# One core, hybrid mixer and mixture of experts: two-head units on row tiles, halved exponentials, one bank for chunk output and state, another load order at the start

## The chip, the cores and the metric

One core of one Trainium2 chip runs the whole program. The metric is the time of one execution on the device in microseconds (us), as the median of three runs.

## What is computed

One layer on 1024 tokens of width 1024, all in float32. The projections are the sum of three products of two reduced parts each, so that they keep float32 accuracy.

```python
hq, hf, hi, hg, gq, gk, gv, ga, gg = jnp.split(x @ w_in, split_at, axis=-1)
f = lb + (1.0 - lb) * sigmoid(hf)
o_h = chunk_gla(hq * 128 ** -0.5, 1.0 - f, hi, log(f))          # 4 heads, keys of 128
log_a = log_sigmoid(ga @ w_a2 + b_a) / 16                        # ga has rank 16
o_g = chunk_gla(gq * 64 ** -0.5, gk, gv, log_a)                  # 4 heads, keys of 64
o = concat(rms(o_h) * norm_h * silu(hg), rms(o_g) * norm_g * silu(gg))
x = layer_norm(alpha * x + o @ w_out)
x = layer_norm(alpha * x + hierarchical_moe(x))                  # 64 experts, top 2

def chunk_gla(q, k, v, log_g):   # per head: S_t = diag(g_t) S_{t-1} + k_t v_t^T, o_t = q_t S_t
    b = cumsum(log_g)            # inside a chunk
    scores[t, s] = sum_k q[t, k] * exp(b[t, k] - b[s, k]) * k[s, k]      # s <= t
    o = scores @ v + (q * exp(b)) @ S_prev
    S = exp(b_last) * S_prev + (k * exp(b_last - b))^T @ v
```

## The kernel before

Three stages follow each other: the mixer, the output projection with the first norm and the router, and the experts, whose 402 MB of weights pass through a ring of eight buffers. VectorE (DVE), ScalarE (ACT), POOL (GpSimd) and the load queue SP are ordered by a scheduler when the program is built; the order of TensorE (PE) in the mixer is the program's own (line 642).

**Projections.** `queue` (lines 275 to 289) lists blocks of 128 columns of `w_in`. A block (`block`, line 168) computes 128 by 1024 outputs in two halves of 512 tokens, each with 24 matmuls: for each of 8 slices of the contraction the upper part of the weights times the upper part of x (line 176), the upper part times x's lower part (178), and the lower part times x's upper part (180). The block `ga` has 16 columns and takes the same 48 matmuls, with `gah` and `gal` as its weights. `weights` (139) loads the next block's weights and splits them: a rounded copy on ScalarE (155), the rest by a subtraction on VectorE (156). When a half block ends, its evacuation runs: keys to `k_of`, queries to `q_of`, values to `to_rows` (ScalarE copies them to the tile `vt`, line 217, TensorE turns them 20 matmuls later, 222), gates to `gated`. `fill(n)` issues the next n matmuls of the queue and stands between the steps of the recurrence, so that TensorE has work.

**Start.** `first_blocks` (291) loads x transposed, in eight parts of 128 tokens; the first four come in two halves each. `split_x` makes the rounded upper part `xh` on ScalarE (303) and the lower part `xl` on VectorE or POOL (304). The four last parts wait for the buffers of the first four. Then come the two halves of tokens (loop on n), each for two blocks (i); their matmuls are lines 327 to 329.

**Recurrence.** `gla` (397) handles a unit: units 0 to 3 are one head with keys of 128 rows, units 4 and 5 are two heads with keys of 64 rows each. `prepare` (364) makes the log decays `lg` and their sums `P` within chunks of 128 tokens, eight chunks per head. Scores inside a chunk are built in seven levels, which pair blocks of 1, 2, 4 up to 64 tokens. `level` (426) makes scaled keys and queries: two subtractions on POOL (471, 472), one exponential of 128 by 1024 on ScalarE (473), keys (436, or 454 for two heads) and queries (475) on VectorE. For two heads the keys lie in `K2`: each head has its own 32 columns of a block, with zeros in the other head's 64 rows, and one VectorE instruction per head writes them. `scores` (478) then issues matmuls of 32 by 32 results (485, 500), or the last level's (512 for one head, 518 for two), all with 128 rows of contraction; both heads' results lie in one bank. `masked` (417) puts the results of the first five levels together (422, 424).

**Chunks.** After the levels, line 591 loops over the chunks c: the output's part from the state (595), its part from scores (597), the state's update for chunk c + 1 (`state`, 574: matmul in 580, VectorE in 585 or 587), ScalarE's sum of squares (604) and VectorE's copy (605), then `fill(12)`. Output and state take buffers of the pool `ps_ou`, three banks, each a buffer of its own:

```python
            op = ps_ou.tile([128, W], F32, name="ou")
            if c:
                PE.matmul(op, QI[:, cs], states[c - 1][:, :W], start=True, stop=False)
...
            if c < NT - 2:
                state(c + 1)
...
                S.activation(junk, op[:, w], AF.Square, accum_out=ssq[hh][:, c:c + 1])
                V.tensor_copy(osb[hh][:, c], op[:, w])
            next(steps, None)
            fill(n_ch)
```

`next(steps)` runs a piece of the next unit's `prepare`. After the last unit, `fill(1000)` (695) issues the rest of the projections; buffers of the mixer then become those of the output projection's weights and of the first expert weights.

## Time and profile before

| | |
|---|---|
| median of three runs | 1590.79 us (1589.87 to 1592.31) |
| the profiled execution's own time | 1590.95 us |
| its span, first to last instruction | 1589.2 us |
| TensorE busy, over the span | 1428.5 us (90%) |
| VectorE | 782.0 us (49%) |
| ScalarE | 470.5 us (30%) |
| POOL | 401.7 us (25%) |
| mean granted TensorE clock | 0.958 of full speed |
| moved by DMA | 449.15 MB, mean 283 GB/s |

In the profile a matmul of float32 operands appears as two instructions. Matmuls are pipelined, so their durations overlap; the distance from one start to the next is what one costs in a row of them. A wait in brackets behind a row is idle time of that engine, with the instruction that ended it. Shares over the span are averages over stages with different limits; the rows below are from single stages.

### The profile page before, as it was taken

The page shows a single profiled execution, that of the slowest core. Times are in us where ns is not written, and L with a number is a line of the kernel's source. Part 1 is how long each engine was busy: PE and PEld are TensorE (multiplying, and loading weights), DVE is VectorE, ACT ScalarE, POOL GpSimd, SP SyncE. Part 2 cuts the span into 40 slices and gives each one's busy share as a digit, 9 for nine tenths or more (in the row PEclk, how much of TensorE's full clock was granted, in tenths as well). Part 3 has the DMA queues.
Part 4 walks back from the last instruction along what each step waited for, and adds up shares of the span by engine and source line. Part 5 has one row for each costly group of instructions (what it writes and reads, how often), then busy time and mean ns, then how long its engine had stood idle before and what let it go on. Part 6 is the DMA issues. An engine that isn't in the chain of part 4 may idle for free. (4 is left out here: it accounts for less than half of the span.)

```text
span 1589.2 us, 23253 instructions
## 1 busy us (share of the span) xinstructions
PE 1428.5 (90%) x9359; PEld 806.1 (51%) x9359; DVE 782.0 (49%) x1838; ACT 470.5 (30%) x948; POOL 401.7 (25%) x275
## 2 busy tenths in 40 slices
PE   7999999899999998979988989889998889899795
PEld 5777678677778884333333333333334334334332
DVE  5667645667766672435334354244344334433534
ACT  5546444545533243112112112112112112111210
POOL 4524323323202103112112213113113212321230
PEclk9999999999999999988999999998999999999998
DMA  5101011010137257999999999999999999999992
GB/s 167 42 33 35 29 34 35 28 35 28 33 99 307 75 191 300 425 426 426 424 425 427 425 426 426 426 425 427 425 427 426 426 426 426 422 423 425 424 389 84
DMA packets 61680, 449.15 MB, mean 283 GB/s; under 512 B 12160, under 2 KB 20608, under 8 KB 36608
## 3 DMA queue, kind: packets, MB, share of 16 engines
q1 hardware_dynamic: 50768, 430.01, 65.3%
q0 software_dynamic: 9216, 12.61, 2.2%
q10 hardware_dynamic: 1584, 5.01, 0.8%
q8 instruction: 74, 1.21, 0.3%
q14 instruction: 38, 0.31, 0.1%
HBM read 447.58 MB, written 20.97 MB: 295 GB/s over the span
## 5 line engine op out<-in xcount | busy, mean ns | idle before, releaser
L1151 PE MATMUL gu<-w1u,VOA 128*64 128x512 f32 x1024 | 237.1, 606 | 8.7 <-DMA w1u<-in_wu_dram 8.2
L1151 PE MATMUL gu<-w2u,VOA 128*64 128x512 f32 x1024 | 232.6, 599 | 8.1 <-DMA w2u<-in_wu_dram 8.1
L1036 DVE TENSOR_TENSOR sg<-sg,gu 128x512 f32<-128x512 f32 x32 | 22.0, 688 | 430.6 <-PE gu L1151 430.6
L1080 POOL TENSOR_TENSOR VOA<-VOA 128x1024 f32<-128x1024 f32 x32 | 81.1, 2534 | 368.4 <-PE tp L1026 367.0
L176 PE MATMUL pp<-xh,wh 128*128 128x512 f32 x416 | 172.9, 416 | 0.0
L178 PE MATMUL pp<-xl,wh 128*128 128x512 f32 x416 | 165.7, 398 | 0.0
L180 PE MATMUL pp<-xh,wl 128*128 128x512 f32 x416 | 164.7, 396 | 0.0
L1151 PEld LDWEIGHTS gu<-w1u,VOA 128*64 128x64 f32 x1024 | 80.5, 140 | 160.7 <-issue 139.2
L1151 PEld LDWEIGHTS gu<-w2u,VOA 128*64 128x64 f32 x1024 | 77.0, 139 | 157.8 <-issue 143.1
L1175 PE MATMUL yp<-w1u,hT 128*64 128x512 f32 x512 | 127.7, 656 | 0.0
L1175 PE MATMUL yp<-w2u,hT 128*64 128x512 f32 x512 | 122.2, 633 | 0.0
L1029 ACT ACTIVATE VOA<-tp,cols 128x128 f32<-128x128 f32 x256 | 93.0, 470 | 89.9 <-PE tp L1026 89.9
L1026 PE MATMUL tp<-cst,VOA 128*128 128x128 f32 x256 | 46.2, 330 | 77.6 <-DMA VOA<-x1d,gidx 75.5
L1046 ACT COPY hT<-tp 128x512 f32<-128x512 f32 x32 | 18.8, 586 | 326.3 <-PE tp L1044 326.3
L1011 POOL DMA_INDIRECT VOA<-x1d,gidx x32 | 32.5, 1015 | 299.5 <-DMA out_dram<-VOA,oidx 282.1
L471 POOL TENSOR_TENSOR d<-P 128x512 f32<-128x512 f32 x36 | 51.6, 1435 | 199.6 <-DVE ny L88 65.3
L1053 DVE SCALAR_TENSOR_TENSOR y<-yp,gcol,y 128x512 fp32r<-128x512 f32 x64 | 47.2, 748 | 99.5 <-ACT y L1052 99.2
L1052 ACT ACTIVATE y<-yp,gcol 128x512 fp32r<-128x512 f32 x64 | 44.0, 688 | 171.6 <-PE yp L1175 171.6
L176 PEld LDWEIGHTS pp<-xh,wh 128*128 128x128 f32 x416 | 78.9, 190 | 18.2 <-issue 1.9
L180 PEld LDWEIGHTS pp<-xh,wl 128*128 128x128 f32 x416 | 78.9, 190 | 17.3
L178 PEld LDWEIGHTS pp<-xl,wh 128*128 128x128 f32 x416 | 79.1, 190 | 13.6
L1081 POOL TENSOR_TENSOR VOA<-VOA 128x1024 f32<-128x1024 f32 x32 | 79.6, 2489 | 2.5
(272 smaller groups left out, 2213.6 us busy)
## 6 DMA issues: line engine op xcount, KB each, us to landing
w1u<-in_wu_dram SPq DMA_DIRECT2D x32, 2048.0 KB, 26.5
w1u<-in_wd_dram SPq DMA_DIRECT2D x32, 2048.0 KB, 27.8
w2u<-in_wg_dram SPq DMA_DIRECT2D x31, 2048.0 KB, 23.0
w1u<-in_wg_dram SPq DMA_DIRECT2D x30, 2048.0 KB, 22.0
w2u<-in_wd_dram SPq DMA_DIRECT2D x30, 2048.0 KB, 27.5
w2u<-in_wu_dram SPq DMA_DIRECT2D x30, 2048.0 KB, 24.1
wr<-in_wf_dram SPq DMA_DIRECT2D x36, 256.0 KB, 2.6
r<-in_x_dram SPq DMA_DIRECT2D x8, 512.0 KB, 3.7
```

Source lines behind the costliest of these rows:

```text
L176: PE.matmul(ps, hi[:, k], xh[:, k, ts], start=(k == 0), stop=False)
L178: PE.matmul(ps, hi[:, k], xl[:, k, ts], start=False, stop=False)
L180: PE.matmul(ps, lo[:, k], xh[:, k, ts], start=False, stop=(k == KT - 1))
L471: G.tensor_tensor(ev[:, :, 0], ref, Pv[:, :, 0], OP.subtract)
L1026: PE.transpose(tp[:, i], sv[:, half * 4 + i], ident)
L1029: S.activation(xt[:, c], tp[:, i], AF.Identity, bias=cols[:, 42 + c:43 + c], scale=cols[:, 34 + c:35 + c])
L1052: S.mul(yh[:, ns], yps[n], gate_col)
L1053: V.scalar_tensor_tensor(yl[:, ns], yps[n], gate_col, yh[:, ns], op0=OP.mult, op1=OP.subtract)
L1080: E.tensor_tensor(o, o, ln1[0], OP.mult)
L1081: E.tensor_tensor(o, o, ln1[1], OP.add)
L1151: PE.matmul(dst[64 * b:64 * b + 64], xt[:, c, 64 * b:64 * b + 64], utile[6 * p + u + b][:, c], start=(c == 0), stop=(c == KT - 1))
L1175: PE.matmul(yps[n][64 * b:64 * b + 64], hT[:, c, 64 * b:64 * b + 64], utile[6 * p + 4 + b][:, c, n * 512:(n + 1) * 512], start=(c == 0), s ...
```

## The change

The gate block's two weights become one tile of 32 columns, upper and lower part side by side; its product with x's upper and lower part gives 32 rows, which the low-rank matmul sums, as its weights are there twice. `vt` gets a second buffer. Two-head units keep keys and queries in the one-head layout; each head's score matmuls read its 64 rows alone and write a bank of its own (`banks`), one of them from `ps_ou`. The exponential of a level is done in halves, and the keys are made between POOL's two subtractions in the program. Chunk output and the next state's matmul share one buffer of `ps_ou`. At the start, the first halves of four x parts come before their second halves, the first block's weights between them; two of the four upper parts are made on VectorE, all eight lower ones too, after the upper ones; and the first blocks use x's lower part after all products with its upper part. The unchanged rest of each part is left out here.

```diff
-    gah = mc.tile([128, KT, 16], F32R, name="gah")
-    gal = mc.tile([128, KT, 16], F32R, name="gal")
+    gahl = mc.tile([128, KT, 32], F32R, name="gahl")
...
-    zt = g2.tile([128, 512], F32, name="vt", bufs=1)[:, 0:256].bitcast(BF)
+    zt = g2.tile([128, 512], F32, name="vt", bufs=2)[:, 0:256].bitcast(BF)
...
-    K2 = [pers.tile([128, NT * 4, 2, 32], F32, name=f"K2{i}") for i in range(2)]
-    Kb = [k_.rearrange("p b h s -> p (b h s)")[:, :T] for k_ in K2]
+    Kb = [pers.tile([128, T], F32, name=f"Kb{i}") for i in range(2)]
...
-            (S if i == 0 else nc.sync).dma_start(rs[j], queue[i][0][:, j * m:j * m + m])
+            (S if i == j == 0 else nc.sync).dma_start(rs[j], queue[i][0][:, j * m:j * m + m])
...
             for k in range(KT):
-                PE.matmul(ps, hi[:, k], xh[:, k, ts], start=(k == 0), stop=False)
-                yield
-                PE.matmul(ps, hi[:, k], xl[:, k, ts], start=False, stop=False)
-                yield
-                PE.matmul(ps, lo[:, k], xh[:, k, ts], start=False, stop=(k == KT - 1))
-                if k == KT - 1:
-                    queue[i][1](ps, ts)
-                yield
+                terms = [(hi, xh), (hi, xl)] + ([(lo, xh)] if lo is not None else [])
+                for j, (w, x_) in enumerate(terms):
+                    PE.matmul(ps, w[:, k], x_[:, k, ts], start=(k == 0 and j == 0),
+                              stop=(k == KT - 1 and j == len(terms) - 1))
+                    if k == KT - 1 and j == len(terms) - 1:
+                        queue[i][1](ps, ts)
+                    yield
...
-        def load(q, parts):
-            xr[q] = g2.tile([128, KT, 128], F32, name=("osb", "d")[q % 2])
-            for i in range(parts):
-                ks = slice(i * KT // parts, (i + 1) * KT // parts)
-                nc.sync.dma_start(xr[q][:, ks], xT_in[q][:, ks])
-
-        def split_x(q, i, parts, E):
+        def load(q, i, parts):
+            if i == 0:
+                xr[q] = g2.tile([128, KT, 128], F32, name=("osb", "d")[q % 2])
+            ks = slice(i * KT // parts, (i + 1) * KT // parts)
+            nc.sync.dma_start(xr[q][:, ks], xT_in[q][:, ks])
+
+        def upper(q, i, parts, copy):
             ks, ts = slice(i * KT // parts, (i + 1) * KT // parts), slice(q * 128, (q + 1) * 128)
-            S.copy(xh[:, ks, ts], xr[q][:, ks])
-            E.tensor_tensor(xl[:, ks, ts], xr[q][:, ks], xh[:, ks, ts], OP.subtract)
-
-        s0 = weights(0, raw=g1.tile([128, KT, 128], F32, name="lg"), parts=2)
-        for q in range(4):
-            load(q, 2)
-        s1 = weights(1, raw=g1.tile([128, KT, 128], F32, name="P"))
-        s0()
+            return copy(xh[:, ks, ts], xr[q][:, ks])
+
+        def lower(q, i, parts, E):
+            ks, ts = slice(i * KT // parts, (i + 1) * KT // parts), slice(q * 128, (q + 1) * 128)
+            return E.tensor_tensor(xl[:, ks, ts], xr[q][:, ks], xh[:, ks, ts], OP.subtract)
+
+        l0, s0 = weights(0, raw=g1.tile([128, KT, 128], F32, name="lg"), parts=2)
+        for i in range(2):
+            for j, q in enumerate(range(4)):
+                if (i, j) in ((0, 1), (1, 0)):
+                    l0(i)
+                load(q, i, 2)
+        l1, s1 = weights(1, raw=g1.tile([128, KT, 128], F32, name="P"))
+        l1(0), l1(1)
+        for i in range(2):
+            s0(i)
+            for q in range(4):
+                up = upper(q, i, 2, S.copy if q < 2 else V.tensor_copy)
         for i in range(2):
             for q in range(4):
-                split_x(q, i, 2, V if q < 3 else G)
+                order(lower(q, i, 2, V), up, "the upper parts go first")
         for q in range(4, 8):
-            load(q, 1)
+            load(q, 0, 1)
             if q == 4:
-                s1()
-            split_x(q, 0, 1, V if q % 2 else G)
+                s1(0), s1(1)
+            upper(q, 0, 1, S.copy)
+            lower(q, 0, 1, V if q % 2 else G)
...
-                    PE.matmul(ps, hi[:, k], xl[:, k, ts], start=False, stop=False)
-                    PE.matmul(ps, lo[:, k], xh[:, k, ts], start=False, stop=(k == KT - 1))
+                    PE.matmul(ps, lo[:, k], xh[:, k, ts], start=False, stop=False)
+                for k in range(KT):
+                    PE.matmul(ps, hi[:, k], xl[:, k, ts], start=False, stop=(k == KT - 1))
...
-        for t_ in K2 + Qb + Ab + Sg:
+        for t_ in Kb[1:] + Qb[1:] + Ab + Sg:
...
-                r = slice(32 * n, 32 * n + 16)
+                r = slice(32 * n, 32 * n + 32)
...
         if h0 == 4:
-            for k_ in K2:
-                for hh in range(nh):
-                    G.memset(k_[(1 - hh) * dk:(2 - hh) * dk, :, hh], 0.0)
...
-        def masked(sps, li, first):
+        def masked(sps, li):
             m = slice(32 * li, 32 * li + 32)
-            a, s_ = acc.rearrange("p c u t -> p (c u) t"), sps.rearrange("p c u t -> p (c u) t")
-            shape = [128, NT * nh, 32]
-            if first:
-                V.tensor_tensor(a, s_, msk0[:, None, :].to_broadcast(shape), OP.mult)
-            else:
-                V.copy_predicated(a, mski[:, None, m].to_broadcast(shape), s_)
+            shape = [128, NT, 32]
+            for hh in range(nh):
+                if li == 0:
+                    V.tensor_tensor(acc[:, hh], sps[hh], msk0[:, None, :].to_broadcast(shape), OP.mult)
+                else:
+                    V.copy_predicated(acc[:, hh], mski[:, None, m].to_broadcast(shape), sps[hh])
+
+        def banks(shape):
+
+            n = shape[0] * shape[1]
+            return [(ps_sc.tile([128, 512], F32, name="trp") if hh == 0 else ps_ou.tile([128, 512], F32, name="ou"))
+                    [:, :n].rearrange("p (c t) -> p c t", c=shape[0]) for hh in range(nh)]
...
-            Kt, Qt = (Kb if nh == 1 else K2)[flip[0]], Qb[flip[0]]
+            Kt, Qt = Kb[flip[0]], Qb[flip[0]]
...
-                for hh in range(nh):
-                    r = slice(hh * dk, (hh + 1) * dk)
-                    if h <= 16:
-                        n = 16 // h
-                        o = Kt[r, :, hh].rearrange("p b (n two h) -> p b n two h", two=2, h=h)[:, :, :, half]
-                        i0 = kv[r, :, half].rearrange("p (b n) h -> p b n h", n=n)
-                        i1 = e[r].rearrange("p (b n) h -> p b n h", n=n)
...
-                    V.tensor_tensor(o, i0, i1, OP.mult)
+            Kv, Qv, qv, kv, Pv = v4(Kt), v4(Qt), v4(q), v4(k), v4(P)
...
-                keys(0, ep)
-                keys(1, em)
+                V.tensor_tensor(Kv[:, :, 0], kv[:, :, 0], ep, OP.mult)
+                V.tensor_tensor(Kv[:, :, 1], kv[:, :, 1], em, OP.mult)
...
                 G.tensor_tensor(ev[:, :, 0], ref, Pv[:, :, 0], OP.subtract)
+                S.activation(ev[:, :, 0], ev[:, :, 0], AF.Exp, scale=sc)
+                V.tensor_tensor(Kv[:, :, 0], kv[:, :, 0], ev[:, :, 0], OP.mult)
                 G.tensor_tensor(ev[:, :, 1], Pv[:, :, 1], ref, OP.subtract)
-                S.activation(e, e, AF.Exp, scale=sc)
-                keys(0, ev[:, :, 0])
+                S.activation(ev[:, :, 1], ev[:, :, 1], AF.Exp, scale=sc)
                 V.tensor_tensor(Qv[:, :, 1], qv[:, :, 1], ev[:, :, 1], OP.mult)
...
-                sp = ps_sc.tile([128, NT, nh, 32], F32, name="trp")
+                sp = banks([NT, 32])
                 for c in range(NT):
                     for hh in range(nh):
                         for j in range(4):
                             o = c * 128 + 32 * j
-                            PE.matmul(sp[32 * j:32 * j + 32, c, hh], Kt[:, o:o + 32] if nh == 1 else Kt[:, o // 32, hh],
-                                      Qt[:, o:o + 32], start=True, stop=True)
-                masked(sp, li, li == 0)
+                            PE.matmul(sp[hh][32 * j:32 * j + 32, c], Kt[rows[hh], o:o + 32], Qt[rows[hh], o:o + 32],
+                                      start=True, stop=True)
+                masked(sp, li)
...
-                            PE.matmul(sp[u_:u_ + 32, c // 2, hh], Kt[:, o:o + 32] if nh == 1 else Kt[:, o // 32, hh],
-                                      Qt[:, o + 32:o + 64], start=True, stop=True)
+                            PE.matmul(sp[hh][u_:u_ + 32, c // 2], Kt[rows[hh], o:o + 32],
+                                      Qt[rows[hh], o + 32:o + 64], start=True, stop=True)
...
-                sp = ps_sc.tile([128, NT, 64], F32, name="trp")
+                sp = banks([NT, 64])
                 for c in range(NT):
-                    PE.matmul(sp[:, c], Kt[:, 4 * c:4 * c + 2].rearrange("p b h s -> p (b h s)"),
-                              Qt[:, c * 128 + 64:c * 128 + 128], start=True, stop=True)
+                    o = c * 128
+                    for hh in range(nh):
+                        PE.matmul(sp[hh][rows[hh], c], Kt[rows[hh], o:o + 64], Qt[rows[hh], o + 64:o + 128], start=True,
+                                  stop=True)
                 for hh in range(nh):
-                    for b in range(2):
-                        S.copy(A[hh][32 * b:32 * b + 32, :, 64:128], sp[64 * b + 32 * hh:64 * b + 32 * hh + 32])
+                    S.copy(A[hh][0:64, :, 64:128], sp[hh][rows[hh]])
...
-        def state(c):
-
-            up = ps_ou.tile([128, 128], F32, name="ou")
+        def state(c, up):
...
-        state(0)
+        state(0, ps_ou.tile([128, 512], F32, name="ou")[:, 256:384])
         for c in range(NT):
             cs = slice(c * 128, (c + 1) * 128)
-            op = ps_ou.tile([128, W], F32, name="ou")
+            ou = ps_ou.tile([128, 512], F32, name="ou")
+            op = ou[:, :W]
...
             if c < NT - 2:
-                state(c + 1)
+                state(c + 1, ou[:, 256:384])
```

## Rows read from the trace of the kernel before

**Rows 1.** Busy time per stretch: PE, PEld, DVE, ACT, POOL; clock, DMA share, GB/s
```profile
80.00:100.00 20.00, 16.48 (x85) 13.50 (x82) 15.57 (x26) 12.03 (x22) 10.52 (x7) 1.00 0.08 26
...
400.00:420.00 20.00, 17.47 (x450) 14.10 (x449) 19.45 (x30) 10.67 (x14) 10.11 (x9) 1.00 0.09 30
...
480.00:580.00 100.00, 99.99 (x556) 83.16 (x555) 66.30 (x351) 31.95 (x73) 20.97 (x17) 1.00 0.42 165
620.00:1580.00 960.00, 848.71 (x3735) 344.81 (x3731) 394.56 (x794) 174.78 (x383) 218.54 (x123) 0.94 0.98 414
```

**Rows 2.** Waits of TensorE up to 560 us (in total, times, longest)
```profile
PE ou L580 <- DVE Sg L587: 13.6, 11, 1.8
...
PE trp L222 <- ACT vt L217: 4.3, 2, 3.7
...
PE pp L383 <- DVE lg L385: 2.0, 2, 1.4
PE trp L500 <- DVE VOA L623: 1.9, 1, 1.9
...
PE trp L485 <- DVE acc L424: 1.1, 2, 0.8
```

**Rows 3.** Timeline of TensorE at the start (start us, us, engine, line, operation, wait before)
```profile
11.31 0.80 PE L327 MATMUL pp<-xh,wh 128*128 128x512 f32 x1 [4.99 <-DVE xl L304]
...
25.98 0.39 PE L327 MATMUL pp<-xh,wh 128*128 128x512 f32 x1
26.21 0.39 PE L328 MATMUL pp<-xl,wh 128*128 128x512 f32 x1
```

**Rows 4.** Groups of TensorE by form up to 460 us: the gate block
```profile
L178 PE MATMUL pp<-xl,gah 128*16 128x512 f32 x16 | 6.3, 394 | 0.0
```

**Rows 5.** Timeline of TensorE: a score level of each kind, and level 6 of each
```profile
60.61 0.76 PE L485 MATMUL trp<-Qb,K 128*32 128x32 f32 x64
...
408.40 1.30 PE L485 MATMUL trp<-Qb,K 128*32 128x32 f32 x128
...
79.42 0.69 PE L512 MATMUL trp<-Qb,K 128*64 128x64 f32 x16
...
424.63 1.90 PE L518 MATMUL trp<-Qb,K 128*128 128x64 f32 x16
```

**Rows 6.** Timeline of TensorE in the chunks of unit 0
```profile
86.34 0.38 PE L595 MATMUL ou<-Sg,QI 128*128 128x128 f32 x2
...
92.78 0.49 PE L580 MATMUL ou<-VOA,KLt 128*128 128x128 f32 x2 [1.26 <-DVE Sg L587]
...
101.39 0.38 PE L595 MATMUL ou<-Sg,QI 128*128 128x128 f32 x2
```

**Rows 7.** Timeline of VectorE in the same chunks
```profile
97.48 0.33 DVE L587 SCALAR_TENSOR_TENSOR Sg<-Sg,gdec,ou 128x128 f32<-128x128 f32 x1
```

**Rows 8.** Timeline of ScalarE in unit 5's chunks
```profile
437.53 0.28 ACT L604 ACTIVATE junk<-ou 128x128 bf16<-128x128 f32 x1 [1.03 <-DVE osb L605]
```

**Rows 9.** Waits of VectorE up to 460 us (in total, times, longest)
```profile
DVE osb L605 <- ACT junk L604: 20.4, 18, 3.4
```

**Rows 10.** Groups of VectorE by form up to 460 us (count, busy us, mean ns)
```profile
L454 DVE TENSOR_TENSOR K<-k,d 64x512 f32<-64x512 f32 x32 | 30.3, 948 | 1.1 <-PE trp L485 0.5
...
L424 DVE COPY_PREDICATED acc<-mski,trp 128x256 f32<-128x256 int32 x16 | 7.0, 440 | 0.6 <-PE trp L485 0.6
L424 DVE COPY_PREDICATED acc<-mski,trp 128x512 f32<-128x512 int32 x8 | 5.8, 725 | 0.0
...
L304 DVE TENSOR_TENSOR xl<-osb,xh 128x512 fp32r<-128x512 f32 x4 | 2.7, 682 | 0.0
```

**Rows 11.** Timeline of ScalarE at the start: the last part of x
```profile
22.16 1.05 ACT L303 CAST xh<-d 128x1024 fp32r<-128x1024 f32 x1 [0.78 <-DMA d<-in_xT_dram]
```

**Rows 12.** Timeline of ScalarE near 50 us
```profile
48.84 1.06 ACT L473 ACTIVATE d<-d 128x1024 f32<-128x1024 f32 x1 [2.06 <-POOL d L472]
49.80 0.57 ACT L217 COPY vt<-pp 128x512 f32<-128x512 f32 x1
```

More of the change, by code (lines that the diff above doesn't have):

```diff
@@ L141, in weights @@
         if queue[i][0] is None:
-            wts[i] = gah, gal
+            wts[i] = gahl, None
             return
@@ L163, in weights @@
             return
-        for j in range(parts):
-            load(j)
-        return lambda: [split(j) for j in range(parts)]
+        return load, split
     def block(i):
@@ L215, in evac @@
         def evac(ps, ts):
-            vt = g2.tile([128, 512], F32, name="vt", bufs=1)
+            vt = g2.tile([128, 512], F32, name="vt", bufs=2)
             S.copy(vt, ps)
@@ L237, in low_rank @@
             r = ts.start // 8 + 32 * g
-            S.copy(gaT[r:r + 16], ps[:, g * 256:g * 256 + 256])
+            S.copy(gaT[r:r + 32], ps[:, g * 256:g * 256 + 256])
     kq = {}
@@ L403, in gla @@
         W = nh * 128
+        rows = [slice(hh * dk, (hh + 1) * dk) for hh in range(nh)]
         Pc = P.rearrange("p (c i) -> p c i", i=128)
@@ L491, in scores @@
                             d_ = slice(32 * j, 32 * j + 32)
-                            (G.tensor_copy if hh == 0 else S.copy)(A[hh][d_, :, d_], acc[d_, :, hh])
+                            (G.tensor_copy if hh == 0 else S.copy)(A[hh][d_, :, d_], acc[d_, hh])
             elif li == 5:
-                sp = ps_sc.tile([128, 4, nh, 32], F32, name="trp")
+                sp = banks([4, 32])
                 for c in range(NT):
```

22 lines of the change are left out of this document (4 added, 18 removed).

## The prediction

> **What bounds the kernel now.** I read the stretches first [rows 1]. From 620 us on the expert weights stream at a DMA share of 0.98, 414 GB/s, with TensorE waiting in between: nothing before that stretch changes its length, only its start. From 480 to 580 us TensorE is busy 99.99 of 100 us with the leftover projections and the output matmuls. So the mixer's end sets when this tail starts, the tail sets when the stream starts, and a microsecond off TensorE's own sequence before 460 us is a microsecond off the end. Within the mixer TensorE's order is written by hand and its work fixed; what can go is work taken out, and idle time. The stretch 80 to 100 has TensorE busy for 16.48 of 20 us, the stretch 400 to 420 (a two-head unit) for 17.47, with VectorE at 19.45: there VectorE is the bound.
>
> Second, the waits of TensorE up to 560 us [rows 2]. Largest is the state matmul (line 580) waiting for VectorE's state update (line 587): 13.6 us in 11 waits. Then the transposes of v waiting for ScalarE's copy, 4.3; the low-rank gate matmul, 2.0; and in the last unit scores waiting for VectorE, 1.9 and 1.1. Third, the first matmul, at 11.31 us, which waits for x's lower part [rows 3].
>
> **The change part by part.** The profiled execution took 1590.95 us (span 1589.2); the sum is made against it. The median is 0.16 lower, which I neglect. A measurement of this kernel tells a change from none at about 0.2%, 3.2 us.
>
> *Gate block.* Its three matmuls per k become two, since one 32-column weight holds both parts: 16 matmuls less [rows 4] (16 of them). At the pace of matmuls of 512 columns, 0.23 us from start to start [rows 3] (25.98, 26.21), that is 3.7 us of TensorE's own sequence, gone for certain: the columns are counted by the moving side, 512 as before.
>
> *Row tiles.* A score level of a two-head unit is 128 instructions in 1.30 us, one of a one-head unit 64 in 0.76 [rows 5]: 0.54 for the second head. Now the heads lie in different rows and write different banks. If their tiles run side by side, the second head's 0.54 goes; if instructions go through one by one, nothing does; the count is unchanged, so I see no loss. Ten such levels: 0 to 5.4, and I take half, 2.7, since both ends are rows of the same instruction. Level 5 with half as many instructions: 0.3 for both units. Level 6 takes 1.90 us for 16 instructions of 128 by 128 weights; it becomes 32 of 64 by 64, on two tiles. If each costs what one costs now it is 1.9 more per unit; if all go at once in pairs, 0.95 less; at the pace of a one-head level 6 (two column tiles, 16 in 0.69) it is 1.4, 0.5 less, and that row is the nearest: 1.0 for two units. Sum 4.0, ends -4 and 8. The Trainium skill, "TensorEngine Tiling (Array Packing)", Theoretical Speedup, gives up to 2x for a dimension of 64 or less. By that rule this term would be its upper end, 8.0, and the total 1562.8 us. No row before shows a tile of 64 rows.
>
> *Chunk output and state in one bank.* Today the state matmul of chunk c+1 waits until VectorE has read the state of chunk c: at 92.78 after 1.26 us of it [rows 6]. With three banks going round by chunk, it has no such wait. What is late next is the output matmul of chunk c+1, which reads that state a fill later (12 matmuls, 2.8 us). I walk unit 0 [rows 6]. The output of chunk 1 starts at 86.34; a chunk without a wait is about 0.6 of its own matmuls and 2.8 of fill, so chunks 2, 3, 4 would start near 89.8, 93.2 and 97.0 (a transposition lies in the last). VectorE ends the states that chunks 3 and 4 need just before 92.78 [rows 6] and at 97.81 [rows 7]. Only chunk 4 waits, to 97.85, where it now starts at 101.39: 3.5 us won. Later chunks of this unit have no wait now. But VectorE and ScalarE will meet in that bank (next paragraph), so of the 13.6 us and some 1.5 of drains behind them I take two thirds, 10; ends 0 and 15.
>
> *What the shared bank adds.* In a two-head unit ScalarE's square of one head waits for VectorE's copy of the other head, other columns of the same bank: 1.03 us at 437.53 [rows 8]. With the state in that bank the order becomes state update, square, copy: ScalarE's queue stands behind VectorE's, and VectorE's next copy stands behind the square and its read. VectorE waits for squares 20.4 us in 18 waits already [rows 9]. When nothing lies between, one such wait is what a square (0.28 [rows 8]) and the read behind it take, about 0.44. There are 36 chunks with a state of their own. TensorE feels it only through the state update, with 2.8 us of fill as cover; if that cover is gone, it costs 36 x 0.44 = 16 us. I charge it inside the third that I left out. The Trainium skill, "PSUM — Partial Sum Buffer", PSUM bank collisions raise a hardware error, says that two engines may never touch one bank in the same partitions at once, whatever the columns, and must be kept apart by semaphores. The row at 437.53 agrees, and by that rule alone the chain just described is certain while its price is not.
>
> *VectorE in two-head units.* Keys took two instructions of 64 rows, 32 in all at 0.948 us [rows 10]; now 16 of 128 rows, of the same 512 columns: 15 us less of VectorE. The masks cost two of 0.440 instead of one of 0.725 [rows 10], 0.16 a level, 1.6 in all. VectorE gains some 6.5 us per unit, and the waits of 1.9 and 1.1 us sit in unit 5 [rows 2]. I take 2.5; ends 0 and 3.4 with drains. Four POOL memsets go as well; POOL is not what these waits end on.
>
> *First blocks.* The first halves of x now come first, the lower parts of x are used after all the others, and four upper parts move to VectorE. TensorE needs the first five loads to start where it needed nine, which I estimate at 3.5 us before 11.31 [rows 3], at the cost of lower parts later: eight on VectorE behind the last upper part. They also free the buffers for x's second half of rows: the four loads on SP's queue wait for them, and the small loads and the next weights stand behind these. Today the last of these x parts is cast at 22.16 to 23.21 [rows 11] and the second half's first matmul starts at 25.98 [rows 3]. I put VectorE's eight lower parts (0.682 each now [rows 10]) at 11 to 16.5, so the loads end near 22 again; the second half can then start near 23.3 to 23.5. That is 2.5 won; ends -1 (loads later than now) and 4.
>
> *Exponentials in halves, v's copy in two buffers.* Each level's exponential of 1.06 becomes two of about 0.57 (the 128x512 copy below it) [rows 12]: 0.1 more ScalarE for each of 36, hidden, as ScalarE waits for POOL in these places. The v transposes near 50 us wait because ScalarE's queue holds the copy behind an exponential that waits for POOL's second half. Only its second half waits now, so the copy moves by some 0.5 of the 3.7 waited there. With the second v buffer's 0.6 at the other such wait [rows 2] I take 1.0; ends 0 and 4.3. The low-rank gate's 2.0 us wait [rows 2] may ease as VectorE does: 0.5, ends 0 and 3.
>
> Sum: 3.7 + 4.0 + 10 + 2.5 + 2.5 + 1.0 + 0.5 = 24.2 us. 1590.95 - 24.2 = 1566.7 us.
>
> **The rivals.**
> *The wait only changes its name.* The bank's order, state, square, copy, holds VectorE, and the output matmul waits for the state where the state matmul did. For it: VectorE is 15.57 busy in 80 to 100 and waits for squares. Against: a fill of cover. The chunk term is 0: 1576.7 us.
> *Nearly all idle time goes.* Row tiles at 8.0, chunks 15, start 4, VectorE 3.4, v 3, the gate block 3.7, low rank 1.5: 38.6, 1552.3 us. Against: the start is set by loads and the wait near 50 us by POOL.
> *Slower.* The 16 us of the shared bank fall on TensorE's path, the 13.6 stay, and of the gains only the gate block and 2 us of scores are real: +10.3, 1601.2 us. It decides where VectorE has no gap left within a chunk; a stretch with 19.45 us in 20 exists [rows 1], but it holds score levels, and the stretch of chunks has a gap of 4.4 us.
> *The change does little:* row tiles go one by one, loads start the second half as late as now, and the chunk waits half stay while squares take the rest: the gate block is all, about 1588 us.
>
> **How the numbers follow.** Forecast 0.53, the renamed wait 0.20, nearly all 0.14, little 0.06, slower 0.07. The forecast with its ends runs from about 1557 to 1576. To leave out no more than two in ten I reach up over the renamed wait and its own spread, to 1583, and down to 1555, leaving out half of the best case and both bad ones. Faster by over 0.2%: forecast, renamed and nearly all, and a little of the fourth, 0.88; within 0.2%: 0.05; slower: 0.07.
>
> **What would show it.** The gate block with 32 matmuls instead of 48; a two-head level under 1.3 us, near 1.0; no wait of line 580's successor on the state update, and waits, if any, on the output matmul; keys as 16 instructions of 128x512; the first matmul near 7.7 us and the second half near 23.4; the stretch after 620 as long as now. Wrong it would be if the stream's start did not move with the mixer's end, or if squares waiting for state updates filled ScalarE's waits while TensorE's chunks grew beyond 3.5 us.

## The result and the profile after

The changed kernel takes 1576.92 us (median of four runs, 1574.96 to 1580.0), the kernel before, run beside it, 1591.53: ratio 0.9908, with an interval of 0.9897 to 0.992. That is 14.6 us faster. The profiled execution took 1576.06 us.

The page of the changed kernel, first two lines:

```profile
span 1574.3 us, 23282 instructions
PE 1417.3 (90%) x9375; PEld 796.3 (51%) x9375; DVE 761.5 (48%) x1838; ACT 473.4 (30%) x976; POOL 391.9 (25%) x267
```

The stretches that answer to [rows 1], each laid where the same work now stands (columns as there):

```profile
80.00:100.00 20.00, 19.13 (x102) 15.93 (x101) 15.76 (x26) 12.23 (x24) 10.52 (x7) 1.00 0.08 27
385.00:405.00 20.00, 16.44 (x442) 13.40 (x440) 15.18 (x27) 8.38 (x12) 9.16 (x10) 0.91 0.10 29
465.00:565.00 100.00, 99.99 (x556) 83.14 (x554) 67.22 (x351) 30.81 (x72) 20.94 (x17) 1.00 0.41 160
605.00:1565.00 960.00, 844.58 (x3737) 340.94 (x3733) 384.23 (x794) 174.20 (x383) 221.22 (x123) 0.94 0.98 414
```

The tail and the stream are what they were; they only start earlier. The chunks of unit 0 went from 16.48 busy to 19.13 of 20 us. The two-head levels of unit 5 went the other way, 17.47 to 16.44, and VectorE is no longer full there (19.45 to 15.18): something else makes TensorE wait, and TensorE's clock is 0.91 there, where it was 1.00.

The waits of TensorE up to 560 us (in total, times, longest), answering to [rows 2]:

```profile
PE trp L217 <- ACT vt L212: 3.4, 4, 1.1
PE trp L473 <- DVE acc L428: 3.2, 1, 3.2
PE pp L333 <- DVE xh L298: 3.0, 2, 1.7
...
PE ou L584 <- DVE Sg L575: 2.7, 2, 1.6
PE trp L488 <- DVE VOA L612: 2.4, 1, 2.4
PE pp L174 <- DVE wl L154: 1.9, 1, 1.9
PE pp L390 <- DVE lg L392: 1.8, 2, 1.1
PE pp L336 <- DVE xl L302: 1.7, 3, 1.2
PE trp L473 <- DVE acc L426: 1.5, 1, 1.5
PE pp L333 <- ACT xh L298: 1.3, 1, 1.3
```

The 13.6 us on the state update have become 2.7, now at the output matmul (line 584). New are waits of scores for VectorE (lines 428, 426, 612), of a projection for a weight's lower part (154), and in the first blocks.

Where the time came from is read off TensorE's timelines: the start of the first score of a unit (S) and of its first state product (C). The first line gives the kernel before, in us; the others are shifts against it, for the change and for runs told below (each from its one profiled execution).

| | S0 | C0 | S1 | S2 | C3 | S4 | S5 | C5 | first output matmul |
|---|---|---|---|---|---|---|---|---|---|
| before | 56.5 | 82.9 | 118.4 | 180.9 | 277.9 | 317.9 | 393.8 | 429.3 | 476.0 |
| changed | -4.2 | -1.2 | -4.4 | -7.4 | -12.3 | -13.6 | -17.0 | -14.2 | -14.8 |
| shared bank alone | -0.1 | -0.1 | -2.7 | -5.4 | -6.0 | -4.0 | -7.6 | -3.4 | -3.4 |
| gate block alone | 1.3 | 1.4 | 1.4 | 1.4 | -3.1 | -3.2 | -3.8 | -3.8 | -3.8 |
| row tiles alone | -4.1 | 0.5 | 0.6 | 0.6 | 0.5 | 2.3 | 3.2 | -0.4 | -1.2 |
| halves alone | -3.2 | 0.2 | 0.2 | 0.2 | 0.2 | 4.3 | 4.4 | 5.4 | 5.3 |
| changed, own banks | -2.6 | -1.4 | -1.4 | -1.0 | -5.4 | -4.7 | -2.8 | -3.9 | -4.8 |
| changed, old loads | -5.6 | -0.9 | -4.0 | -6.9 | -11.7 | -12.9 | -17.3 | -13.3 | -14.1 |

The chunks of units 0 and 1 (C0 to S1, and in S1 to S2) win 3.2 and 3.0 us, those of units 3 and 4 1.3 and 2.5; the gate block's matmuls leave in unit 2. Two stretches give time back: the levels of unit 0 (S0 to C0) 3.0, and those of unit 5 (S5 to C5) 2.9.

Part of these shifts is not waiting but TensorE's clock. The next table has, from the same executions, the length of a stretch in us, TensorE's busy time in it, and the mean granted clock (1.00 is 2.4 GHz; the lower level is 1.2). The matmuls of a stretch are nearly the same in every row, so length less busy time is waiting, and more busy time at a lower clock is slower matmuls.

| | chunks of unit 3 (C3 to S4) | chunks of unit 4 (to S5) | levels of unit 5 (S5 to C5) |
|---|---|---|---|
| before | 40.0, 34.3, 1.00 | 43.3, 39.6, 0.96 | 35.4, 32.3, 1.00 |
| changed | 38.7, 35.3, 0.96 | 40.7, 38.1, 1.00 | 38.3, 32.7, 0.96 |
| shared bank alone | 42.0, 35.2, 0.96 | 40.0, 37.9, 1.00 | 39.7, 33.3, 0.96 |
| row tiles alone | 41.7, 36.8, 0.92 | 45.0, 41.0, 0.92 | 31.9, 31.5, 1.00 |
| halves alone | 44.0, 38.2, 0.88 | 43.6, 39.3, 0.96 | 36.5, 32.2, 1.00 |
| changed, own banks | 40.7, 35.5, 0.96 | 47.1, 42.4, 0.89 | 34.4, 31.5, 1.00 |
| changed, one normalization chain | 38.7, 35.3, 0.96 | 40.8, 39.4, 0.96 | 37.5, 34.3, 0.91 |

In unit 5's levels the changed kernel waits 2.5 us more than the one before, and at 0.96 its matmuls take 1.3 us longer than at 1.00 in the run with row tiles alone.

### The profile page after: what moved, and what is told of

It is laid out like the page before. It is cut to its first block, busy times and chain, and to the rows that moved or that the text cites. A ratio compares the mean times of both kernels' runs of the same rounds, so it can differ in the third digit from the quotient of the medians.

```text
span 1574.3 us, 23282 instructions
## 1 busy us (share of the span) xinstructions
PE 1417.3 (90%) x9375; PEld 796.3 (51%) x9375; DVE 761.5 (48%) x1838; ACT 473.4 (30%) x976; POOL 391.9 (25%) x267
## 5 line engine op out<-in xcount | busy, mean ns | idle before, releaser
L1140 PE MATMUL gu<-w2u,VOA 128*64 128x512 f32 x1024 | 234.0, 600 | 10.5 <-DMA w2u<-in_wu_dram 10.5
L1140 PEld LDWEIGHTS gu<-w1u,VOA 128*64 128x64 f32 x1024 | 76.1, 139 | 168.5 <-issue 148.2
L1164 PE MATMUL yp<-w2u,hT 128*64 128x512 f32 x512 | 117.8, 614 | 0.0
L174 PEld LDWEIGHTS pp<-xl,wh 128*128 128x128 f32 x416 | 78.9, 190 | 13.7
```

The costliest lines, as they stand in the source:

```text
L174: PE.matmul(ps, w[:, k], x_[:, k, ts], start=(k == 0 and j == 0), stop=(k == KT - 1 and j == len(terms) - 1))
L1140: PE.matmul(dst[64 * b:64 * b + 64], xt[:, c, 64 * b:64 * b + 64], utile[6 * p + u + b][:, c], start=(c == 0), stop=(c == KT - 1))
L1164: PE.matmul(yps[n][64 * b:64 * b + 64], hT[:, c, 64 * b:64 * b + 64], utile[6 * p + 4 + b][:, c, n * 512:(n + 1) * 512], start=(c == 0), s ...
```

## The experiments

Times are medians; differences are to the kernel before run beside it (1590.81, then 1590.55, then 1591.01 us) or to the changed kernel's 1576.92. Intervals of the ratios are about 0.001 to 0.0017 to either side. So a difference to the kernel before is told from none at 1.4 to 2.7 us, and one between two variants of the changed kernel, with four executions each, only at about 3 us.

**One part alone.** Output and state in one bank tile:

```diff
-            up = ps_ou.tile([128, 128], F32, name="ou")
-            op = ps_ou.tile([128, W], F32, name="ou")
+            ou = ps_ou.tile([128, 512], F32, name="ou")
+            op = ou[:, :W]
-                state(c + 1)
+                state(c + 1, ou[:, 256:384])
```

> The kernel before with one part of the change: chunk output and state share a bank tile, so the ring of three is passed once a chunk. Theory A (the chunk ring is the large gain, as the two traces read: about 3.2 + 3.0 us in units 0 and 1, 1.5 and 1.3 in units 2 and 3, 1.5 in unit 4): 10 us faster than before, 1581 to 1583. Rival B (the ring only names a wait on the VectorE and ScalarE chain behind it; the chunks became shorter in the changed kernel because of the other parts): 0 to 4 us faster, 1587 to 1591.

1588.51 us, ratio 0.9987 (0.9978 to 0.9996): 2.3 us. By the total, rival B; but the waits for the state update did go. In its chunks and levels from 80 to 450 us TensorE waits, largest first:

```profile
PE trp L222 <- ACT vt L217: 8.2, 4, 4.4
PE trp L485 <- DVE acc L424: 4.5, 1, 4.5
...
PE ou L595 <- DVE Sg L586: 1.7, 1, 1.7
```

The state update's waits are 2.7 us (1.7 and one of 1.0), but v's copy has 8.2 in their place and the scores 4.5. The table says where: units 0 and 1 gain 2.7 each, the chunks of unit 3 *lose* 2.0 (C3 to S4), and the levels of unit 5 take 4.2 back (each time 1.0 of it by a lower clock). In unit 3's chunks (its timeline, all engines), while unit 4 is being prepared:

```profile
292.33 1.04 POOL L471 TENSOR_TENSOR d<-P 128x512 f32<-128x512 f32 x1 [2.03 <-DVE K L454]
292.60 1.31 DVE L454 TENSOR_TENSOR K<-k,d 64x512 f32<-64x512 f32 x1
293.33 1.72 POOL L472 TENSOR_TENSOR d<-P 128x512 f32<-128x512 f32 x1
...
294.20 1.39 DVE L454 TENSOR_TENSOR K<-k,d 64x512 f32<-64x512 f32 x1
...
295.62 0.69 DVE L475 TENSOR_TENSOR Qb<-q,d 128x512 f32<-128x512 f32 x1
...
296.46 1.04 POOL L471 TENSOR_TENSOR d<-P 128x512 f32<-128x512 f32 x1 [1.42 <-ACT junk L604]
...
297.46 2.13 POOL L472 TENSOR_TENSOR d<-P 128x512 f32<-128x512 f32 x1
...
299.62 1.06 ACT L473 ACTIVATE d<-d 128x1024 f32<-128x1024 f32 x1 [3.23 <-POOL d L472]
300.58 0.57 ACT L217 COPY vt<-pp 128x512 f32<-128x512 f32 x1
...
301.20 0.69 PE L222 MATMUL trp<-cst,vt 128*128 128x128 f32 x2 [4.42 <-ACT vt L217]
```

The key product of a two-head unit is two instructions of 64 rows (line 454); here both run beside POOL and take 1.31 and 1.39 us, where 0.69 is what one takes without it. The next differences start late on POOL (296.46; the profile puts this second wait down to ScalarE's square), ScalarE's queue stands 3.23 us behind them at the exponential, and v's copy stands behind the exponential. That is what TensorE waits for. In the changed kernel the same chain has one key product of 128 rows, and POOL does not pause:

```profile
285.12 1.48 POOL L458 TENSOR_TENSOR d<-P 128x512 f32<-128x512 f32 x1
...
286.57 1.27 POOL L461 TENSOR_TENSOR d<-P 128x512 f32<-128x512 f32 x1
...
287.80 2.02 POOL L458 TENSOR_TENSOR d<-P 128x512 f32<-128x512 f32 x1
...
292.26 0.58 ACT L212 COPY vt<-pp 128x512 f32<-128x512 f32 x1
...
292.90 0.33 PE L217 MATMUL trp<-cst,vt 128*128 128x128 f32 x1 [1.09 <-ACT vt L212]
```

Gate block in two terms with 32 columns:

```diff
-                PE.matmul(ps, lo[:, k], xh[:, k, ts], start=False, stop=(k == KT - 1))
+                terms = [(hi, xh), (hi, xl)] + ([(lo, xh)] if lo is not None else [])
```

> The kernel before with the low-rank gate block in two terms and 32 columns: 16 matmuls fewer. Theory A: their time is on the path, 3.6 us faster (1587.5 to 1588.5). Rival B: the fill work only moves and what comes after waits for VectorE instead: under 1.5 us faster.

1586.54 us, ratio 0.9975 (0.9964 to 0.9986): 4.3 us, theory A. The profile has 4.5 us of it between S2 and C3 (1.4 to -3.1), and it lasts to the end.

Row tiles and masks by head, exponentials whole:

```diff
-                            PE.matmul(sp[32 * j:32 * j + 32, c, hh], Kt[:, o:o + 32] if nh == 1 else Kt[:, o // 32, hh],
-                                      Qt[:, o:o + 32], start=True, stop=True)
+                            PE.matmul(sp[hh][32 * j:32 * j + 32, c], Kt[rows[hh], o:o + 32], Qt[rows[hh], o:o + 32],
+                                      start=True, stop=True)
```

> The kernel before with row tiles and per-head masks in the two-head units, exponentials whole. Theory A (a level of 64 two-head scores costs the same by its count of instructions, 1.22 us against 1.23; levels 5 and 6 give 0.6 to 0.7 us a unit; the rest of the two-head units is set by the VectorE queue): within 2 us of before, 1588.5 to 1592.5. Rival B (my forecast: row tiles and shorter VectorE work together worth 6.5 us): 1584 to 1586. Rival C (one mask instruction a head instead of one in all, and the key product in one instruction, stretch the VectorE queue of unit 5): 2 to 4 us slower than before, 1593 to 1596.

1589.01 us, ratio 0.9985 (0.9976 to 0.9994): 1.8 us, theory A by the number. By the table it is two things that nearly cancel: the levels of units 4 and 5 win 0.8 and 3.6, the chunks of units 3 and 4 lose 1.8 and 1.8. TensorE's waits for the whole mixer still begin with the ring:

```profile
PE ou L561 <- DVE Sg L568: 13.8, 8, 4.2
```

Eight waits in place of eleven, but the longest 4.2 in place of 1.8 [rows 2], and the clock is 0.92 in the chunks of both units: in unit 3 the whole loss is busy time, 36.8 for 34.3 us. So neither part pays alone: the shared bank on the kernel before meets v's copy, the row tiles on it meet the ring. That it is the short key product which clears the way for the shared bank is read from the traces and not tested by a run of these two parts together. The other candidates but one were undone in the changed kernel (below), the second v buffer, the halves and the load order, and none cost anything that shows; the gate block was not undone.

Exponentials in halves:

```diff
-                S.activation(e, e, AF.Exp, scale=sc)
-                keys(0, ev[:, :, 0])
+                S.activation(ev[:, :, 0], ev[:, :, 0], AF.Exp, scale=sc)
+                keys(0, ev[:, :, 0])
+                G.tensor_tensor(ev[:, :, 1], Pv[:, :, 1], ref, OP.subtract)
+                S.activation(ev[:, :, 1], ev[:, :, 1], AF.Exp, scale=sc)
```

> The kernel before with the exponentials of each level in halves and nothing else. Theory A (an activation of half the size costs 0.63 us against 1.06, so two cost 0.2 us more of ScalarE a level, while the keys are ready a POOL instruction earlier; the levels are set by VectorE, so little follows): within 1.5 us of before. Rival B (between the halves other work with another function table gets in, as at 395 us of the changed kernel, where a Silu and two table loads stood between the halves and the second came 3.7 us late): 2 to 4 us slower. Rival C (the forecast, an earlier key product): 1 to 3 us faster.

1594.77 us, ratio 1.0024 (1.0015 to 1.0033): 4.0 us slower, in the size of rival B. Its place is not rival B's, though: all 4 us are lost in the chunks of unit 3, where the longest wait for the state update rises to 3.4 us; unit 5's levels lose 1.0. The loss in unit 3 is not waiting: TensorE is idle for 5.8 us there, before for 5.7, but it is busy for 3.9 us longer with the same work at a clock of 0.88 (these chunks before, then with halves: stretch, PE busy, clock, DMA share, GB/s):

```profile
277.92:317.88 39.96, 34.28 (x174) 1.00 0.09 28
```

```profile
278.12:322.12 44.00, 38.22 (x173) 0.88 0.09 26
```

Behind the long wait, matmuls that start 0.23 us apart at the higher clock start 0.43 apart, up to 311.85:

```profile
306.13 0.80 PE L581 MATMUL ou<-VOA,KLt 128*128 128x128 f32 x2 [3.37 <-DVE Sg L588]
...
307.15 0.63 PE L178 MATMUL pp<-xl,wh 128*128 128x512 f32 x1
307.58 0.63 PE L180 MATMUL pp<-xh,wl 128*128 128x512 f32 x1
```

A second slow stretch, from 281.30 to 284.79, follows a gap of only 0.64 us; why the clock fell there, and why the state update came later, stays open.

**One part undone in the changed kernel.** The second v buffer (`bufs=2` back to `bufs=1`):

> The changed kernel with one vt buffer, as before the change. Theory A (in the kernel with the shared bank alone the waits for Sg fell from 13.6 to 2.7 us in the chunks, but waits for vt rose from 0.6 to 8.2 us; the shared bank pays only with the second vt buffer beside it): vt waits back at about 8 to 11 us, the kernel 4 to 7 us slower than the changed one, 1581 to 1584. Rival B (the vt wait there is only the next wait in line and the same chain ends the chunks anyway): within 1.5 us of the changed kernel, 1575.5 to 1578.5.

1576.91 us: rival B, nothing. The v waits are the same four, 3.4 us. What they wait for is ScalarE's queue, not the buffer. Theory A falls: it is not the second buffer that lets the shared bank pay.

The state's own bank again:

```diff
+            up = ps_ou.tile([128, 128], F32, name="ou")
```

> The changed kernel with a bank tile of its own for the state, as before. Theory A: the waits for Sg at the start of a chunk come back (13 to 14 us of the chunks), about 8 to 10 us slower than the changed kernel, 1585 to 1587. Rival B (the shared bank is worth what it was worth alone, 2.3 us): 1578 to 1580.

1586.77 us, 9.9 us slower than the changed kernel: theory A. The waits from 80 to 450 us begin again with the state update:

```profile
PE ou L569 <- DVE Sg L576: 15.0, 9, 3.2
```

So the same edit is worth 2.3 us on the kernel before and 9.9 on the changed one. Not all of the 9.9 is the wait itself: the chunks of unit 4 are 6.4 us longer with the state's own bank, and 4.3 of these are busy time at a clock of 0.89.

Whole exponentials:

```diff
-                S.activation(ev[:, :, 0], ev[:, :, 0], AF.Exp, scale=sc)
-                S.activation(ev[:, :, 1], ev[:, :, 1], AF.Exp, scale=sc)
+                S.activation(e, e, AF.Exp, scale=sc)
```

> The changed kernel with the exponentials of a level in one instruction, as before. Theory A (halves cost 4.0 us on the kernel before, and cost the same here, since five of the eight table loads of a level now fall between its halves): 3 to 5 us faster than the changed kernel, 1572 to 1574. Rival B (with the lighter key product of the row tiles the VectorE queue takes the early half at once, so that halves pay here): 1 to 4 us slower than the changed kernel, 1578 to 1581. Rival C: within 1 us.

1575.46 us (1572.48 to 1578.93), ratio 0.9895 (0.988 to 0.9911): 1.5 us faster, within the scatter. The number lies in no theory's range; it speaks against B, and a scatter of this size leaves A and C open. Its profiled execution is 2.9 us *longer* than the changed kernel's, because TensorE's clock was granted differently at the start, a mix of its levels of 1.2 and 2.4 GHz (stretch, PE busy, clock, DMA share, GB/s):

```profile
5.00:15.00 10.00, 7.15 (x20) 0.70 1.01 328
15.00:25.00 10.00, 8.10 (x34) 0.95 0.57 210
25.00:35.00 10.00, 9.80 (x36) 0.83 0.01 2
```

The changed kernel has 1.00 in all three. Single executions differ by that much, which is why the medians decide here.

Three key and query tiles of a level in place of two (with one v buffer, for room):

```diff
-    Kb = [pers.tile([128, T], F32, name=f"Kb{i}") for i in range(2)]
+    Kb = [pers.tile([128, T], F32, name=f"Kb{i}") for i in range(3)]
-            flip[0] ^= 1
+            flip[0] = (flip[0] + 1) % 3
```

> The changed kernel with three key and query tiles of a level in place of two, and one vt buffer (both do not fit in the memory together), so it is read against the run with one vt buffer. Theory A (the levels of unit 5 lost 3.4 us because the VectorE products of level 2 stand behind the scores of level 0, and those of level 4 behind these): 2 to 4 us faster than the run with one vt buffer. Rival B (the products wait in the VectorE queue behind the normalization and the exponentials' two tiles, not for the scores): within 1 us of it.

1586.44 us, 9.5 us slower than the run with one v buffer: no theory had that. Unit 5's levels do shrink (33.2 us from S5 to C5, 39.2 with one v buffer, 38.3 in the changed kernel), but in the chunks v's copy is late again:

```profile
PE trp L217 <- ACT vt L212: 10.8, 6, 4.3
```

This is the kind of wait that the shared bank alone has. That the third tile lets more of the next unit's work stand in ScalarE's queue ahead of v's copy is my reading; the run shows the wait, not that order.

The first blocks' loads, splits and terms as before:

```diff
-            for j, q in enumerate(range(4)):
-                if (i, j) in ((0, 1), (1, 0)):
-                    l0(i)
-                load(q, i, 2)
+        for q in range(4):
+            load(q, 2)
```

> The changed kernel with the loads, splits and term order of the first two blocks as before. Theory A (the first 96 matmuls of the first two blocks end 1.96 us earlier in the changed kernel and nothing takes that back before the chunks): 2 us slower than the changed kernel, 1578 to 1580. Rival B (what is gained there is lost in the levels of unit 0, whose scores wait for VectorE in any case; 4.23 us at their start had become 1.20 at their end): within 1 us of it, 1576 to 1578. Rival C (the early start only trades waits): up to 2 us faster.

1575.95 us, ratio 0.9904 (0.9888 to 0.9921): rival B by the number. The new order brings nothing to the end that these runs can tell. It starts earlier, but TensorE then waits in pieces (its timeline in the changed kernel, which answers to [rows 3]):

```profile
7.99 0.47 PE L333 MATMUL pp<-xh,wh 128*128 128x512 f32 x1 [1.66 <-DVE xh L298]
...
11.40 0.47 PE L333 MATMUL pp<-xh,wh 128*128 128x512 f32 x1 [1.33 <-DVE xh L298]
...
16.12 1.20 PE L336 MATMUL pp<-xl,wh 128*128 128x512 f32 x4 [1.21 <-DVE xl L302]
...
24.02 0.50 PE L333 MATMUL pp<-xh,wh 128*128 128x512 f32 x1 [1.26 <-ACT xh L298]
```

The second half of the rows starts at 24.02 in place of 25.98, and the first 96 matmuls end 1.3 us earlier (35.70 for 37.02). This is lost by the end of unit 0's levels: with the old order C0 comes 0.3 us later, not 2, and the first output matmul 0.7. The early S0 of the changed kernel is not the loads' work: with the old order S0 comes earlier still (-5.6), and with row tiles alone, whose start is as before, at -4.1.

**Two tries at more.** Heads alternating for every block of 32:

```diff
-                    for hh in range(nh):
-                        for j in range(4):
+                    for j in range(4):
+                        for hh in range(nh):
```

> The changed kernel, whose two-head scores of levels 0 to 4 go head by head for every block of 32 in place of four blocks of a head after one another: neighbouring matmuls then use the two halves of the rows. Theory A (a level of 64 scores is set by its count of instructions, 19 ns each; their order does not matter): a level at 1.2 to 1.25 us, time within 1 us of the changed kernel. Rival B (two row tiles work at once only where neighbours differ in their rows): a level at 0.65 to 0.8 us, 2 to 5 us faster. Rival C (neighbours on the same columns wait for one another's results): a level at 1.6 to 2.5 us, up to 6 us slower.

A level is the same, the changed kernel's first and the alternating one's second (stretch of one level, PE busy and count of that line, clock, DMA share, GB/s):

```profile
381.00:382.60 1.60, 1.29 (x128) 1.00 0.13 41
```

```profile
381.00:382.60 1.60, 1.29 (x128) 1.00 0.17 60
```

Theory A on the level. The time is 1573.53 us (1573.29 to 1574.55), ratio 0.9893 (0.9876 to 0.9909). That is 3.4 less than the changed kernel, with overlapping intervals, and A did not expect it: the 2.4 us wait at level 5 of unit 5 is 0.4 here. In the changed kernel that wait is made by a weight's split ahead of the queue:

```profile
404.08 0.62 ACT L153 CAST wh<-wr 128x512 fp32r<-128x512 f32 x1 [3.95 <-DMA wr<-in_wf_dram]
...
404.73 0.69 DVE L154 TENSOR_TENSOR wl<-wr,wh 128x512 fp32r<-128x512 f32 x1 [1.86 <-ACT wh L153]
405.34 0.68 DVE L463 TENSOR_TENSOR Qb<-q,d 128x512 f32<-128x512 f32 x1
...
406.30 0.68 DVE L612 TENSOR_SCALAR VOA<-trp,cols 128x512 f32<-128x512 f32 x1
407.03 0.22 PE L488 MATMUL trp<-Qb,Kb 64*32 64x32 f32 x2 [2.42 <-DVE VOA L612]
```

A weight's transfer is late, ScalarE's cast waits for it, VectorE stands idle 1.86 us behind the cast, and the copy that frees a bank for the scores stands behind VectorE's query product. In the alternating kernel this split is not ahead of it and the copy starts at 404.11. The same thing stands in unit 0: VectorE waits 3.47 us at 57.20 for a cast, and the scores behind its mask (line 426) wait 1.46.

One normalization chain for both heads of a unit:

```diff
-            rs = rstd_of(small, ssq[hh], NT, "n")
+        ry = rstd_of(small, sf, nh * NT, "n").rearrange("p (h c) -> p h c", h=nh)
```

> The changed kernel with one normalization chain for both heads of a unit: 12 small VectorE instructions fewer in unit 4 and in unit 5, at 0.1 to 0.2 us each. Theory A (the levels of unit 5 wait 3.2 and 2.4 us for a VectorE queue in which the two normalization chains, their two products and the halves of another gate stand; unit 5 took back 3.4 us of what PE had gained): 2 to 3.5 us faster than the changed kernel, 1573.5 to 1575, with the 3.2 us wait at the third level of unit 5 down to 1 to 2 us. Rival B (what ends that wait is the chain from one level's products over POOL's differences to the next one's exponentials, 3.4 us a level): within 1 us. Rival C (head 0 now waits for head 1's last square, so its turn comes later): up to 2 us slower.

1576.66 us, ratio 0.991 (0.9893 to 0.9926): rival B on the time. The 3.2 us wait fell to 1.3 and the 2.4 to 0.8, but waits of 1.1 for the normalized product came, and unit 5's levels shrank by only 0.8 us, which the stage before had lost. TensorE does wait less in these levels, 3.2 us for 5.6, about what theory A forecast; but it is busy 1.6 us longer, at a clock of 0.91 for 0.96. So this profile shows the waits shorter and most of the gain lost to the clock.

The same with whole exponentials in unit 5 alone:

> As the run with the joint normalization, with whole exponentials in unit 5 alone, where the levels took 36.1 us with whole exponentials and 38.3 with halves (from the start of the scores to the first state product), and halves in units 0 to 4. Theory A (in unit 5 the half with the table loads before it comes late): 1 to 2.5 us faster than the run with the joint normalization alone, 1571.5 to 1573.5. Rival B (the two kernels' executions differ by a clock that was granted otherwise at the start, and halves or whole make no difference): within 1 us of it.

1573.3 us (1571.84 to 1574.04), ratio 0.9886 (0.987 to 0.9903): the fastest, 3.4 below the joint normalization alone and 3.6 below the changed kernel. All its runs lie below all of the changed kernel's, though the intervals of the two ratios overlap a little. The time lies in A's range, but A's place is not shown: unit 5's levels take 37.4 us here and 37.5 in the run with the joint normalization alone. What made the difference stays open.

## Why the prediction was right, and where it was not

The forecast was 1566.7 us, faster; it became 1576.92, inside the range and faster, but 10 us short. It lies on the number of the renamed wait (1576.7), whose mechanism is not what happened: the range held it because it reached up over that rival, and that is luck. Of the 24.2 us forecast, the bank and the gate block brought what they were to bring, 14.2 for 13.7; the other terms, 10.5 us together, leave 0.4 beside them. No term stood for TensorE's clock, which was lower behind long waits.

- *Gate block, 3.7:* right; 4.3 alone.
- *Chunk output and state in one bank, 10:* right in size, 9.9 when undone, and the walk of unit 0 held: 3.5 forecast, 3.2 won. It failed as a term that stands by itself: alone it is 2.3. The step "of the 13.6 us I take two thirds" left out who is late next in unit 3, v's copy behind ScalarE's exponentials, and that slow matmuls can follow a long wait: part of the 9.9 is clock.
- *What the shared bank adds:* the chain state, square, copy is there (VectorE waits 26.2 us in 32 waits for squares, where [rows 9] has 20.4 in 18) and costs nothing that shows at TensorE in units 0 and 1; the fill covers it. Squares of the changed kernel wait 17.9 us in 16 waits for the state update in their bank. The Trainium skill, "PSUM — Partial Sum Buffer", PSUM bank collisions raise a hardware error, wants engines kept apart by semaphores in one bank; these waits agree, and no run here shows a collision. The price, which I had left to the rivals, is at most the 2.7 us that TensorE still waits for state updates.
- *Row tiles, 4.0:* wrong. Levels 0 to 4 got nothing, 1.29 for [rows 5]'s 1.30. "I take half, 2.7, since both ends are rows of the same instruction" was a choice between two mechanisms, and it was the other: so many instructions take so long, whatever their rows, and in whatever order. Level 6 got 0.75 a unit (1.15 for 1.90), more than the 0.5 forecast, but not by its rows: neighbouring matmuls now use different columns of the array too, as they do in the one-head level 6 with all 128 rows [rows 5]. Less the 0.22 us that the last one takes, 16 instructions in 0.69 there and 32 in 1.15 here are 0.029 each, the same pace. Twice 0.69, the forecast's 1.4, counted that last part twice. So 1.6 or so of the 4.0, level 5's 0.06 a unit (0.76 for 0.82) with it. The Trainium skill, "TensorEngine Tiling (Array Packing)", Theoretical Speedup, gives up to 2x for a dimension of 64 or less; no run here shows such a gain from tiles of 64 rows.
- *VectorE in two-head units, 2.5:* the place was wrong. Alone, row tiles shorten unit 5's levels by 3.6; in the changed kernel they are 2.9 longer. My reading is that TensorE comes 17 us earlier and the chain of normalization, products, differences and exponentials does not; it fits the run with own banks, where TensorE comes 14 us later and these levels take 34.4, and 1.3 us are the clock's. Where it paid, by the traces, is the chunks of unit 3, as the condition for the shared bank.
- *First blocks, 2.5:* 2.0 won where the second half starts, near the 2.5 walked, then lost: nothing that shows at the end, by the run that undoes it. The step failed that let a gain before unit 0's levels pass through them: 1.3 was left after the first blocks, and three waits for VectorE (1.91, 1.46, 0.87 us) took it and most of what the wait near 50 us had cost.
- *Halves and v's copy, 1.0:* v's second buffer 0; halves not told apart from nothing in the changed kernel, and 4.0 slower alone, a sign that my bounds (0 to 4.3) excluded; in the profile those 4.0 are slower matmuls.
- *Low-rank gate, 0.5:* 0.2; the waits are 1.8 for 2.0.

By the runs, the bank's 9.9 (undone in the changed kernel) and the gate block's 4.3 (alone) make 14.2 of the 14.6 us; the four parts tried alone sum to 4.4. The rest of the parts seems to be worth what it does for the bank.

## What to carry to other kernels

A wait that is taken away is worth what the second latest input allows, and that input can differ from stage to stage: walk each stage with the wait gone, not one for all. Parts that clear the way for one another can only be priced together; undoing a part in the finished kernel tells more of its worth there than doing it alone. A wait of a few us can cost again in slower matmuls behind it: before a loss is put down to waiting, compare busy time and granted clock of the same stretch. In an in-order queue, an instruction that waits for a transfer should not stand ahead of one that frees a bank for TensorE.

## What the runs showed of the hardware

A VectorE product of a level that starts while POOL is in a subtraction mostly ends about 0.55 us after that subtraction: with the shared bank alone, 292.60 + 1.31 and 294.20 + 1.39 against POOL's ends at 293.37 and 295.05, and 0.69 when POOL is idle (295.62). So nearly all of the product runs once POOL is through, and all but some 0.15 us of what is left of POOL's instruction is added, not a share. From 40 to 460 us, 38 of 39 such products in that run do this and 31 of 35 in the changed kernel, of those that start more than 0.14 us before POOL's end; the others went first and ended before POOL did. The Trainium skill, "SBUF — State Buffer", Who interferes with whom, calls the shared port pair an exclusive lock; these rows agree.

Matmuls of 64 by 64, whose two heads use different rows and different columns, run side by side in pairs (level 6 of unit 5, timeline):

```profile
411.21 0.22 PE L508 MATMUL trp<-Qb,Kb 64*64 64x64 f32 x1
411.22 0.22 PE L508 MATMUL ou<-Qb,Kb 64*64 64x64 f32 x1
411.27 0.22 PE L508 MATMUL trp<-Qb,Kb 64*64 64x64 f32 x1
411.28 0.22 PE L508 MATMUL ou<-Qb,Kb 64*64 64x64 f32 x1
```

The two heads start 0.01 us apart, the next pair 0.06 later. That is the pace of weights of 128 by 64 in the one-head level 6 (0.029 us an instruction in both), so the different columns are enough for it. With 32 columns, 128 instructions take 1.29 us, 0.010 each, with one row tile or two: there the time goes by the count of instructions. Each has a weight load of its own, and whether the matmul or the load sets this pace the runs do not tell.

TensorE's matmuls of 512 columns start 0.23 us apart at a clock of 1.00, and 0.43 apart after the 3.37 us wait above, for some 5 us.
